# Block products of a Strassen FFN merged in TensorE's accumulators, and norms ahead of weights in the order of work

## The chip, the cores and the metric

The kernel runs on one core of a Trainium2 chip. The metric is the device time of one execution in microseconds (us): the median of three runs before is 1083.9 us (1083.37 to 1085.91). Five engines work side by side, each through a list of instructions of its own, in order: TensorE (PE; matmuls into accumulator tiles called `ps`), VectorE (DVE), ScalarE (ACT), GpSimd (POOL) and SyncE (SP, which issues DMAs). An instruction that needs the result of another engine waits for a semaphore.

## The reference

Two layers over 512 tokens of width 1024, in float32. Each layer has a mixer (attention and pooling in the first, a gated recurrence in the second) and then a SwiGLU FFN, both with a norm ahead and a norm behind:

```
D_MODEL = 1024; SEQ = 512; DEPTH = 2; D_FF = 2816

def rmsnorm(x, g):
    return x * lax.rsqrt(jnp.mean(x * x, axis=-1, keepdims=True) + RMS_EPS) * g

def swiglu(h, w_gate, w_up, w_down):
    return (jax.nn.silu(h @ w_gate) * (h @ w_up)) @ w_down

def reference(x, ...):
    for layer in range(DEPTH):
        h = rmsnorm(x, mix_pre_g[layer])
        m = even_mixer(h, ...) if layer % 2 == 0 else odd_mixer(h, ...)
        x = x + rmsnorm(m, mix_post_g[layer])
        h = rmsnorm(x, ffn_pre_g[layer])
        x = x + rmsnorm(swiglu(h, w_gate[layer], w_up[layer], w_down[layer]), ffn_post_g[layer])
    return x
```

## The kernel before, in words

**Precision.** Every float32 operand is split into a high and a low part, and a product is made of three matmuls (`mm3`: high x high, high x low, low x high). A unit of weights (128 x 1024) is loaded by SyncE into `raw`; ScalarE casts its high part into `whi`, and VectorE subtracts for the low part, `wlo` (`split_weights`). There are four buffers each of `whi` and `wlo`, used in turn.

**The FFN's first half.** The gate and up products are computed by a Strassen-Winograd scheme of 2 x 2 blocks: token blocks 0 and 1 against 2 and 3, and the two halves of the width. The normed and transposed tokens are kept in seven slots of features: `A11` and `A12` (blocks 0 and 1), `S1` to `S4` and `A22`, which need blocks 2 and 3. The output has `NP` = 11 tiles j, and each takes seven block products, one for each slot, with seven units of weights (some are sums of raw weights that VectorE makes). `gate_product` is one block product: 24 matmuls of 256 columns into one accumulator. The results are then merged by additions and subtractions (`y`, `z`, `c`), and `gated` forms silu(gate) x up out of each of the four quarters: a silu on ScalarE and a multiplication on VectorE.

For the first `LEAD` = 5 tiles A11 and A12 are computed early ("led"), while blocks 2 and 3 still go through the norm; the copy of A11's result is kept in a later part of `gs` meanwhile. Then the loop over all j computes S1, S2, (for j from 5 on A11 ahead of these and A12 behind S2), S3, S4 and A22.

**The norms.** `Finish` takes a mixer's output by token blocks of 128. `half` makes the squares on ScalarE (`Square`, with a sum) and the product with the gain on VectorE; `block` adds the residual and makes the squares for the next norm; `second`, some us later, the normed block `tmp`; `transpose`, later again, eight transposes on TensorE, whose results `Blocks.put` splits into the seven slots. `later(delay, ...)` and `tick` put these steps at a place in the program by a running count of matmul time; `need` waits for blocks.

**The order of work.** A scheduler orders each engine's instructions. What stands in `tc.high_priority` goes ahead of work that was written earlier, if its inputs are there by the scheduler's reckoning. Before the change only weights (loads, casts, splits, sums of raw weights) have it.

Lines of the profile that matter: L158 the cast to `whi`, L867 the copy of A11's result to `y`, L857 the silu, L705 the squares of `half`, L722 those of `block`, L743 the transposes, L136 to L138 the three matmuls of `mm3`. All of VectorE's instructions have line L100.

Of the kernel before, what the change touches and what calls it, by code (L numbers as in the profile page):

```python
# [15 lines left out]
P = 128  # L16
# [13 lines left out]
WINDOWS = (2, 4, 8, 16)  # L30
OUT_ORDER = (0, 1, 2, 7, 6, 5, 3, 4)


WARM = 8
ON_DVE = (0, 2)
# [29 lines left out]
def tile_trunk(ctx: ExitStack, tc: tile.TileContext, cst_d, sh_d, xw_d, x_d, gains_d, pw_d, w_d, out_d):  # L65
# [13 lines left out]
    def ps():  # L79
        return psp.tile([P, T], F32, name="ps", tag="ps")  # L80
# [29 lines left out]
    def tmp():  # L110
        return pc.tile([P, D], F32, name="tmp", tag="tmp", bufs=3)
# [6 lines left out]
    def later(delay, fn):  # L118
        pending.append((clock[0] + delay, fn))
        pending.sort(key=lambda p: p[0])  # L120
# [33 lines left out]
        return raw[:, :n]  # L154

    def split_weights(raw, hi, lo):
        with tc.high_priority():
            nc.scalar.copy(out=hi, in_=raw)  # L158
            vec.tensor_sub(out=lo, in0=raw, in1=f32(hi))

    def add_to(acc, other, eng):
        with tc.high_priority():
            eng.tensor_add(out=acc, in0=acc, in1=other)


# [473 lines left out]
    class Plain:  # L639


        def put(self, i, tps):
            for hf, tp in enumerate(tps):
                tv = tp.rearrange("p (k t) -> p k t", k=4)
                ks = slice(4 * hf, 4 * hf + 4)
                nc.scalar.copy(out=hBh[:, i, ks], in_=tv)
                vec.tensor_sub(out=hBl[:, i, ks], in0=tv, in1=f32(hBh[:, i, ks]))

    class Blocks:


        def put(self, i, tps):
            cs = slice(i % 2 * P, i % 2 * P + P)
# [29 lines left out]
    class Finish:  # L683
# [12 lines left out]
        def half(self, i, hf, acc, made_by=None):  # L696

            if i not in self.u:
                self.u[i] = (small(2), tmp())
            ss, u = self.u[i]  # L700
            cs = slice(hf * T, (hf + 1) * T)
            if made_by is not None:
                made_by(u[:, cs])
                acc = u[:, cs]
            nc.scalar.activation(out=junk[:, cs], in_=acc, func=AF.Square, scale=1.0 / 32, accum_out=ss[:, hf:hf + 1])  # L705
            vec.tensor_mul(out=u[:, cs], in0=acc, in1=self.gpost[:, cs])

        def block(self, i):
            ss, u = self.u.pop(i)
            gpre = self.gpre  # L710
            r = rstd(ss, 2)
            x = xres[i]
            halves = [slice(0, T), slice(T, D)]
            parts = halves if i == NB - 1 else [slice(0, D)]
            s2 = small(2)
            for q, cs in enumerate(parts):
                vec.scalar_tensor_tensor(out=x[:, cs], in0=u[:, cs], scalar=r, in1=x[:, cs], op0=ALU.mult,
                                               op1=ALU.add)
                if gpre is None:
                    nc.sync.dma_start(out=out_d[i * P:(i + 1) * P, cs], in_=x[:, cs])  # L720
                else:
                    nc.scalar.activation(out=junk[:, cs], in_=x[:, cs], func=AF.Square, scale=1.0 / 32,  # L722
                                         accum_out=s2[:, q:q + 1])
            if gpre is None:
                return
            box = {}

            def second():
                r2 = rstd(s2, len(parts))
                h = box["h"] = tmp()  # L730
                for cs in halves:
                    vec.scalar_tensor_tensor(out=h[:, cs], in0=x[:, cs], scalar=r2, in1=gpre[:, cs],
                                                   op0=ALU.mult, op1=ALU.mult)
                later(T1 if i < NB - 1 else T2, transpose)

            def transpose():
                h = box["h"]
                tps = []
                for hf in range(2):
                    tp = ps()  # L740
                    for b in range(4):
                        k = 4 * hf + b
                        nc.tensor.transpose(tp[:, b * P:(b + 1) * P], h[:, k * P:(k + 1) * P], ident)  # L743
                    tps.append(tp)
                self.sink.put(i, tps)
                made.add(i)

            made.discard(i)
            later(T3, second)
# [80 lines left out]
    def ffn(layer):  # L830
        st = ExitStack()
        pf = st.enter_context(tc.tile_pool(name=f"ffn{layer}", bufs=1, reuse_waits="tile"))
        upper[:] = [pf.tile([P, KT // 2 * D], F32R, name=f"up{n}") for n in range(2)]

        def ytile():
            return pf.tile([P, T], F32, name="y", tag="y", bufs=2)

        def gt(dt=F32):
            return pf.tile([P, 2, T], dt, name="g", tag="g", bufs=NP)


        gs = [gt() for _ in range(NP)]

        def gate_product(bank, w, f, more=False):
            wh, wl = w
            fh, fl = slot(f)
            for g in range(2):
                for k in range(4):
                    cs = slice(g * T + k * P, g * T + k * P + P)
                    ts = slice(k * 256, k * 256 + 256)  # L850
                    mm3(bank[:, g * 256:g * 256 + 256], wh[:, cs], wl[:, cs], fh[:, ts], fl[:, ts],
                        not more and g == 0 and k == 0, g == 1 and k == 3, 0.356, more)

        def gated(j, f, src, s):

            gate, up = src[:, :256], src[:, 256:]
            nc.scalar.activation(out=s, in_=gate, func=AF.Silu)  # L857
            cs = slice(f % 2 * 256, f % 2 * 256 + 256)
            vec.tensor_mul(out=gs[j][:, f // 2, cs], in0=s, in1=up)

        def first(j):

            b1 = ps()
            gate_product(b1, unit(), A11)

            y = gs[NP - 1 - j][:, 1] if j < LEAD else ytile()
            nc.scalar.copy(out=y, in_=b1)  # L867
            return b1, y

        def second(j, b1):  # L870
            gate_product(b1, unit(), A12, True)
            gated(j, 0, b1, tmp()[:, :256])

        led = []
        need(0, 1)
        for j in range(LEAD):
            led.append(first(j))
            second(j, led[j][0])
        need(2, 3)
        for j in range(NP):  # L880
            b1, y = led[j] if j < LEAD else first(j)
            z, c = hx[:, j % 2, :T], hx[:, j % 2, T:]
            b3 = ps()
            gate_product(b3, unit(), S1)
            b2 = ps()
            gate_product(b2, unit(), S2)
            vec.tensor_add(out=y, in0=b2, in1=y)
            vec.tensor_sub(out=z, in0=b3, in1=y)
            if j >= LEAD:
                second(j, b1)  # L890
            b4 = ps()
            gate_product(b4, unit(), S3)
            vec.tensor_sub(out=c, in0=z, in1=b4)
            gated(j, 3, c, c[:, :256])
            b5 = ps()
            gate_product(b5, unit(), S4)
            vec.tensor_add(out=z, in0=b5, in1=z)
            gated(j, 2, z, z[:, :256])
            gate_product(b4, unit(), A22, True)
            vec.tensor_add(out=y, in0=b4, in1=y)  # L900
            gated(j, 1, y, y[:, :256])


        def area(a):
            t = (hh, hl_) + tuple(upper)
            per = KT * T // D
            t = t[a // per]
            return tuple(t[:, a % per * D + n * T:a % per * D + n * T + T] for n in range(2))

        TAIL = 6  # L910
        early = [11, 15, 2, 6, 3, 7, 0, 4, 1, 5]
        areas = early + early[:FT - TAIL - len(early)] + [8, 12, 9, 13, 10, 14]
        parts = []

        def part(k, ahead=2):
            while len(parts) < min(FT, k + 1 + ahead):
                n = len(parts)
                src = gs[n // 2][:, n % 2]
                hi, lo = area(areas[n])
                nc.scalar.copy(out=hi, in_=src)  # L920
                vec.tensor_sub(out=lo, in0=src, in1=f32(hi))
                parts.append((hi, lo))
            return parts[k]

        for n in range(4):
            place[state["used"] + FT - TAIL + n] = lambda: tuple(gt(F32R).rearrange("p a t -> p (a t)") for _ in range(2))
        tm = TokenMajor([lambda k=k: part(k) for k in range(FT)], TAIL)
        tm.lead(range(3), (0, 1))
        tm.lead(range(3), (2, 3))
        tm.lead(range(3, FT - TAIL), range(NB))  # L930
        fin = Finish(1 if layer == 0 else 3, Plain())
        prefetch(TAIL + 2)
        tm.finish(range(NB), fin)
        st.close()
# [183 lines left out]
```

## Time and profile before

| | |
|---|---|
| median of three runs | 1083.9 us |
| the profiled execution's own time | 1087.36 us |
| its span, first to last instruction | 1085.6 us |
| TensorE busy | 1041.1 us, 96% |
| VectorE busy | 768.8 us, 71% |
| ScalarE busy | 516.9 us, 48% |
| mean granted clock of TensorE | 0.988 |

The busy share of an engine is a mean over stretches that differ. In the FFNs TensorE has no idle time for long stretches; in the transitions from mixer to FFN (about 190 to 240 us in layer 0, 720 to 760 us in layer 1) it waits for others. So a change has to be read stretch by stretch.

### The profile page before, as it was taken

The page shows a single profiled execution, that of the slowest core. Times are in us where ns is not written, and L with a number is a line of the kernel's source. Part 1 is how long each engine was busy: PE and PEld are TensorE (multiplying, and loading weights), DVE is VectorE, ACT ScalarE, POOL GpSimd, SP SyncE. Part 2 cuts the span into 40 slices and gives each one's busy share as a digit, 9 for nine tenths or more (in the row PEclk, how much of TensorE's full clock was granted, in tenths as well). Part 3 has the DMA queues.
Part 4 walks back from the last instruction along what each step waited for, and adds up shares of the span by engine and source line. Part 5 has one row for each costly group of instructions (what it writes and reads, how often), then busy time and mean ns, then how long its engine had stood idle before and what let it go on. Part 6 is the DMA issues. An engine that isn't in the chain of part 4 may idle for free. (4 is left out here: it accounts for less than half of the span.)

```text
span 1085.6 us, 16315 instructions
## 1 busy us (share of the span) xinstructions
PE 1041.1 (96%) x6558; PEld 931.0 (86%) x6558; DVE 768.8 (71%) x1045; ACT 516.9 (48%) x815; POOL 60.7 (6%) x96
## 2 busy tenths in 40 slices
PE   8989999789999999999999999897999999999997
PEld 6867777789999999888898887687999999988886
DVE  3778875788998989432357589468899889963313
ACT  6747644654444446332245894355444444542301
POOL 0020100100000000000012102210000000000000
PEclk9989999899999999999999999998999999999999
DMA  8563353232443244334123234132442432443201
GB/s 320 170 146 83 107 171 120 98 114 101 156 131 104 80 139 131 113 108 150 57 75 101 84 110 152 26 115 97 148 141 101 129 105 80 136 135 98 98 1 77
DMA packets 36188, 125.08 MB, mean 115 GB/s; under 512 B 4368, under 2 KB 4368, under 8 KB 36112
## 3 DMA queue, kind: packets, MB, share of 16 engines
q1 hardware_dynamic: 35536, 121.94, 35.6%
q10 hardware_dynamic: 576, 2.10, 0.5%
q8 instruction: 51, 0.84, 0.3%
q14 instruction: 25, 0.20, 0.1%
HBM read 117.73 MB, written 2.10 MB: 110 GB/s over the span
## 5 line engine op out<-in xcount | busy, mean ns | idle before, releaser
L158 ACT CAST whi<-raw 128x1024 fp32r<-128x1024 f32 x230 | 239.0, 1047 | 310.4 <-PE ps L137 113.1
L100 DVE TENSOR_TENSOR wlo<-raw,whi 128x1024 fp32r<-128x1024 f32 (+1 forms) x238 | 286.3, 1212 | 124.7 <-ACT whi L158 119.6
L136 PE MATMUL ps<-hTh,whi 128*128 128x256 f32 (+1 forms) x960 | 294.6, 307 | 5.5 <-ACT whi L158 2.5
L138 PE MATMUL ps<-hTh,wlo 128*128 128x256 f32 (+1 forms) x960 | 294.0, 307 | 3.8 <-DVE wlo L100 3.8
L137 PE MATMUL ps<-hTl,whi 128*128 128x256 f32 (+1 forms) x960 | 292.2, 305 | 3.5 <-DVE hTl L100 3.5
L136 PEld LDWEIGHTS ps<-hTh,whi 128*128 128x128 f32 x960 | 182.7, 190 | 15.0 <-ACT whi L158 3.1
L138 PEld LDWEIGHTS ps<-hTh,wlo 128*128 128x128 f32 x960 | 182.4, 190 | 13.3 <-DVE wlo L100 4.6
L137 PEld LDWEIGHTS ps<-hTl,whi 128*128 128x128 f32 x960 | 182.8, 190 | 12.2 <-DVE hTl L100 3.7
L136 PE MATMUL ps<-up,whi 128*128 128x256 f32 x528 | 149.8, 284 | 2.2 <-DVE hx L100 2.1
L137 PE MATMUL ps<-up,whi 128*128 128x256 f32 x528 | 149.4, 283 | 0.0
L138 PE MATMUL ps<-up,wlo 128*128 128x256 f32 x528 | 149.2, 283 | 0.0
L100 DVE TENSOR_TENSOR raw<-raw 128x1024 f32<-128x1024 f32 x88 | 106.9, 1220 | 8.1 <-DMA raw<-in_w 7.8
L136 PEld LDWEIGHTS ps<-up,whi 128*128 128x128 f32 x528 | 101.1, 191 | 3.1 <-DVE hx L100 3.0
L137 PEld LDWEIGHTS ps<-up,whi 128*128 128x128 f32 x528 | 101.2, 192 | 0.0
L138 PEld LDWEIGHTS ps<-up,wlo 128*128 128x128 f32 x528 | 101.1, 192 | 0.0
L100 DVE TENSOR_TENSOR tmp<-ps,gain 128x512 f32<-128x512 f32 x32 | 21.9, 690 | 59.0 <-ACT junk L705 58.9
L636 POOL TENSOR_TENSOR small<-small,nhalf 128x1 f32<-128x1 f32 x28 | 15.4, 549 | 800.1 <-DVE small L100 800.1
L137 PE MATMUL ps<-wlo,hTh 128*128 128x512 f32 (+2 forms) x160 | 55.8, 352 | 3.2 <-DVE wlo L100 3.1
L138 PE MATMUL ps<-whi,hTl 128*128 128x512 f32 (+2 forms) x160 | 55.5, 350 | 0.0
L136 PE MATMUL ps<-whi,hTh 128*128 128x512 f32 (+2 forms) x160 | 54.3, 351 | 0.6 <-ACT whi L303 0.6
L705 ACT ACTIVATE junk<-ps 128x512 bf16<-128x512 f32 x32 | 19.0, 596 | 60.7 <-PE ps L138 60.2
L138 PE MATMUL ps<-whi,hTh 128*128 128x512 f32 x96 | 38.0, 396 | 0.0
(220 smaller groups left out, 1655.3 us busy)
## 6 DMA issues: line engine op xcount, KB each, us to landing
raw<-in_w SPq DMA_DIRECT2D x200, 512.0 KB, 3.8
gain<-in_gains SPq DMA_DIRECT2D x7, 512.0 KB, 4.2
raw<-in_xw SPq DMA_DIRECT2D x6, 516.0 KB, 9.1
big<-in_x ACTq DMA_DIRECT2D x4, 512.0 KB, 7.8
big<-big SPq DMA_DIRECT2D x16, 128.0 KB, 4.2
xres<-in_x SPq DMA_DIRECT2D x4, 512.0 KB, 5.0
out_dram<-xres SPq DMA_DIRECT2D x3, 512.0 KB, 2.6
big<-tmp SPq DMA_DIRECT2D x8, 128.0 KB, 3.9
```

Of the source, the lines that this page charges most:

```text
L100: self.last = fn(*a, **k)
L136: nc.tensor.matmul(out, lhsT=ah, rhs=bh, start=start, stop=False, skip_group_check=more)
L137: nc.tensor.matmul(out, lhsT=ah, rhs=bl, start=False, stop=False, skip_group_check=more)
L138: nc.tensor.matmul(out, lhsT=al, rhs=bh, start=False, stop=stop, skip_group_check=more)
L158: nc.scalar.copy(out=hi, in_=raw)
L636: nc.gpsimd.tensor_tensor(out=r, in0=ms, in1=nhalf[:, :1], op=ALU.pow)
L705: nc.scalar.activation(out=junk[:, cs], in_=acc, func=AF.Square, scale=1.0 / 32, accum_out=ss[:, hf:hf + 1])
```

## The change

The merges move in part from VectorE into the accumulators. Two accumulators, `bw` and `bz`, are kept for the whole loop over j. ScalarE copies A11's result into `bw`, and S2 accumulates on it; ScalarE copies the negative of that into `bz`, and S3 and then A22 accumulate on `bw`, S4 on `bz`. VectorE keeps two merges of five for each j (`c` and `z`), ScalarE makes three copies (to `bw`, `bz`, `y`) in place of one, or of none for the led tiles, whose copy was made early. Two matmuls for each layer write the two accumulators once ahead of the loop. The norms of `Finish` get high priority, that of weights is set to 1500 places (`AHEAD`), and the transposes before an FFN are put 2.5 us later by the program's own count (`delay`).

```diff
+AHEAD = 1500
...
     def split_weights(raw, hi, lo):
-        with tc.high_priority():
+        with tc.high_priority(AHEAD):
...
     class Blocks:
+        delay = 2.5
...
         def half(self, i, hf, acc, made_by=None):
...
-            nc.scalar.activation(out=junk[:, cs], in_=acc, func=AF.Square, scale=1.0 / 32, accum_out=ss[:, hf:hf + 1])
-            vec.tensor_mul(out=u[:, cs], in0=acc, in1=self.gpost[:, cs])
+            with tc.high_priority():
+                nc.scalar.activation(out=junk[:, cs], in_=acc, func=AF.Square, scale=1.0 / 32,
+                                     accum_out=ss[:, hf:hf + 1])
+                vec.tensor_mul(out=u[:, cs], in0=acc, in1=self.gpost[:, cs])
         def block(self, i):
+            with tc.high_priority():
+                self._block(i)
...
-        led = []
         need(0, 1)
         for j in range(LEAD):
-            led.append(first(j))
-            second(j, led[j][0])
+            b1 = first(j)
+            nc.scalar.copy(out=gs[NP - 1 - j][:, 1], in_=b1)
+            second(j, b1)
         need(2, 3)
+        bw, bz = ps(), ps()
+        for b in (bw, bz):
+            nc.tensor.matmul(b, lhsT=junk[:, :P], rhs=junk[:, :T], start=True, stop=True)
         for j in range(NP):
-            b1, y = led[j] if j < LEAD else first(j)
-            z, c = hx[:, j % 2, :T], hx[:, j % 2, T:]
-            b3 = ps()
-            gate_product(b3, unit(), S1)
-            b2 = ps()
-            gate_product(b2, unit(), S2)
-            vec.tensor_add(out=y, in0=b2, in1=y)
-            vec.tensor_sub(out=z, in0=b3, in1=y)
+            if j < LEAD:
+                nc.scalar.copy(out=bw, in_=gs[NP - 1 - j][:, 1])
+            else:
+                b1 = first(j)
+                nc.scalar.copy(out=bw, in_=b1)
+            b5 = ps()
+            gate_product(b5, unit(), S1)
+            y = ytile()
+            nc.scalar.copy(out=y, in_=b5)
+            gate_product(bw, unit(), S2, True)
+            nc.scalar.mul(out=bz, in_=bw, mul=-1.0)
             if j >= LEAD:
                 second(j, b1)
-            b4 = ps()
-            gate_product(b4, unit(), S3)
-            vec.tensor_sub(out=c, in0=z, in1=b4)
+            z, c = hx[:, j % 2, :T], hx[:, j % 2, T:]
+            gate_product(bw, unit(), S3, True)
+            vec.tensor_sub(out=c, in0=y, in1=bw)
             gated(j, 3, c, c[:, :256])
-            b5 = ps()
-            gate_product(b5, unit(), S4)
-            vec.tensor_add(out=z, in0=b5, in1=z)
+            gate_product(bz, unit(), S4, True)
+            vec.tensor_add(out=z, in0=y, in1=bz)
             gated(j, 2, z, z[:, :256])
-            gate_product(b4, unit(), A22, True)
-            vec.tensor_add(out=y, in0=b4, in1=y)
-            gated(j, 1, y, y[:, :256])
+            gate_product(bw, unit(), A22, True)
+            gated(j, 1, bw, tmp()[:, :256])
```

**Where instructions stand, first place: the loop at j = 6, layer 0.** On ScalarE before, around the copy of A11's result (`y_3614` <- `ps_3582`); `whi_3648` and `whi_3679` are the weights of S3 and S4 of this j, and the second of these casts waits for S1's last matmul but one, which reads the buffer before:

```order
L857 ACTIVATE y_3385<-y_3385 128x256 [waits DVE_49]
L158 CAST whi_3648<-raw_3550 128x1024 [waits PE_49,Activation_49]
L867 COPY y_3614<-ps_3582 128x512 [waits PE_49]
L158 CAST whi_3679<-raw_3585 128x1024 [waits DMAHW1_49,PE_49,Activation_49]
L158 CAST whi_3711<-raw_3517 128x1024 [waits DVE_49,PE_49,Activation_49]
L158 CAST whi_3744<-raw_3746 128x1024 [waits DMAHW3_49,PE_49,Activation_49]
```

After, at the same place, with `whi_3644` and `whi_3674` for S3 and S4; `ps_2521` is `bw`, `ps_2522` is `bz`:

```order
L870 ACTIVATE tmp_3575<-ps_2521 128x256 [waits PE_49]
L160 CAST whi_3644<-raw_3546 128x1024 [waits PE_49,Activation_49]
L160 CAST whi_3674<-raw_3581 128x1024 [waits DMAHW1_49,PE_49,Activation_49]
L900 COPY ps_2521<-ps_3578 128x512 [waits DVE_49,Activation_49]
L904 COPY y_3642<-ps_3611 128x512 [waits PE_49]
L160 CAST whi_3705<-raw_3513 128x1024 [waits PE_49]
L907 ACTIVATE ps_2522<-ps_2521 128x512 [waits PE_49,Activation_49]
```

The copy to `bw` stands behind both casts, where the copy to `y` stood between them. On TensorE before, where S1 ends (`ps_3616`) and S2 begins (`ps_3647`); the waits at S2 are for its weights:

```order
L138 MATMUL ps_3616<-hTh_65,wlo_3549 128x256
L136 MATMUL ps_3616<-hTh_65,whi_3548 128x256
L137 MATMUL ps_3616<-hTl_66,whi_3548 128x256
L138 MATMUL ps_3616<-hTh_65,wlo_3549 128x256
L136 MATMUL ps_3647<-hTh_65,whi_3583 128x256 [waits Activation_49]
L137 MATMUL ps_3647<-hTl_66,whi_3583 128x256
L138 MATMUL ps_3647<-hTh_65,wlo_3584 128x256 [waits DVE_49]
```

After, S2 accumulates in `ps_2521`:

```order
L140 MATMUL ps_3611<-hTh_65,wlo_3545 128x256
L138 MATMUL ps_3611<-hTh_65,whi_3544 128x256
L139 MATMUL ps_3611<-hTl_66,whi_3544 128x256
L140 MATMUL ps_3611<-hTh_65,wlo_3545 128x256
L138 MATMUL ps_2521<-hTh_65,whi_3579 128x256 [waits Activation_49]
L139 MATMUL ps_2521<-hTl_66,whi_3579 128x256
L140 MATMUL ps_2521<-hTh_65,wlo_3580 128x256
```

S2's one wait for ScalarE is now one for the copy to `bw`.

**Second place: a led tile, j = 2 of layer 0.** On ScalarE before, where the casts follow each other (`whi_2886` for S4 and `whi_2917` for A22 of this j, `whi_2952` for S1 of the next):

```order
L158 CAST whi_2856<-raw_2789 128x1024 [waits PE_49,Activation_49]
L158 CAST whi_2886<-raw_2823 128x1024 [waits DMAHW1_49,PE_49,Activation_49]
L158 CAST whi_2917<-raw_2787 128x1024 [waits DVE_49,PE_49,Activation_49]
L857 ACTIVATE hx_67<-hx_67 128x256 [waits DVE_49]
L158 CAST whi_2952<-raw_2954 128x1024 [waits PE_49]
L857 ACTIVATE hx_67<-hx_67 128x256 [waits DVE_49]
L857 ACTIVATE g_2141<-g_2141 128x256 [waits DVE_49]
```

After: `whi_2890` and `whi_2919` are the weights of S4 and A22 of this j, `whi_2953` those of S1 of the next, `ps_2858` is S1's accumulator, `g_2140` holds A11's result:

```order
L160 CAST whi_2890<-raw_2825 128x1024 [waits DMAHW1_49,PE_49]
L870 ACTIVATE tmp_2854<-ps_2521 128x256 [waits PE_49]
L160 CAST whi_2919<-raw_2789 128x1024 [waits PE_49,Activation_49]
L904 COPY y_2888<-ps_2858 128x512 [waits PE_49]
L897 COPY ps_2521<-g_2140 128x512 [waits DVE_49]
L160 CAST whi_2953<-raw_2955 128x1024 [waits PE_49]
L907 ACTIVATE ps_2522<-ps_2521 128x512 [waits PE_49,Activation_49]
L160 CAST whi_2989<-raw_2955 128x1024 [waits DVE_49,PE_49]
```

The copies to `y` and to `bw` stand behind one cast, the copy to `bz` behind the next.

**Third place: the norm of block 3 in layer 0.** On ScalarE before; `xres_1833` is the residual of block 3, `whi_2262` and `whi_2323` are weights of led products:

```order
L158 CAST whi_2204<-raw_2206 128x1024 [waits DMAHW7_49,PE_49]
L705 ACTIVATE junk_68,small_2092<-ps_1949 128x512
L867 COPY g_2142<-ps_2143 128x512 [waits PE_49]
L722 ACTIVATE junk_68,small_2121<-xres_1833 128x512 [waits DMAHW4_49,DVE_49,Activation_49]
L158 CAST whi_2262<-raw_2264 128x1024 [waits DMAHW0_49,PE_49]
L158 CAST whi_2323<-raw_2325 128x1024 [waits DMAHW1_49,PE_49]
L722 ACTIVATE junk_68,small_2121<-xres_1833 128x512 [waits DVE_49,Activation_49]
```

After:

```order
L712 ACTIVATE junk_68,small_2092<-ps_1948 128x512 [waits PE_49,Activation_49]
L712 ACTIVATE junk_68,small_2092<-ps_1949 128x512 [waits PE_49]
L674 COPY hx_67<-ps_2051 128x4x128 [waits DVE_49]
L160 CAST whi_2204<-raw_2206 128x1024 [waits DMAHW7_49,PE_49]
L888 COPY g_2142<-ps_2143 128x512 [waits PE_49]
L734 ACTIVATE junk_68,small_2121<-xres_1833 128x512 [waits DMAHW4_49,DVE_49,Activation_49]
L734 ACTIVATE junk_68,small_2121<-xres_1833 128x512 [waits DVE_49,Activation_49]
L160 CAST whi_2262<-raw_2264 128x1024 [waits DMAHW0_49,PE_49]
```

The second half's squares have moved ahead of both casts. On VectorE after, the rows up to the split of block 3's S1 slot, `hTl_66<-tmp_2321`:

```order
L102 TENSOR_TENSOR wlo_2420<-raw_2421,whi_2419 128x1024 [waits DMAHW4_49,PE_49,Activation_49]
L102 TENSOR_TENSOR tmp_2244<-tmp_2245,hx_67 128x512
L102 TENSOR_TENSOR up1_2131<-tmp_2244,up0_2130 128x4x128
L102 TENSOR_TENSOR g_2133<-tmp_2292,ps_2203 128x256
L102 TENSOR_TENSOR wlo_2454<-raw_2455,whi_2453 128x1024 [waits PE_49,Activation_49]
L102 TENSOR_TENSOR up1_2131<-tmp_2244,up0_2130 128x4x128 [waits Activation_49]
L102 TENSOR_TENSOR raw_2455<-raw_2455,raw_2489 128x1024 [waits DVE_49]
L102 TENSOR_TENSOR raw_2623<-raw_2623,raw_2625 128x1024 [waits DMAHW4_49,DMAHW3_49]
L102 TENSOR_TENSOR tmp_2321<-ps_2311,tmp_2321 128x512 [waits Activation_49]
L102 TENSOR_TENSOR tmp_2322<-hx_67,ps_2311 128x512
L102 TENSOR_TENSOR wlo_2488<-raw_2455,whi_2487 128x1024 [waits PE_49,Activation_49]
L102 TENSOR_TENSOR hTl_66<-tmp_2321,hTh_65 128x4x128 [waits Activation_49]
```

Splits of weights (`wlo`) and sums of raw weights stand in the rows ahead of it.

## Rows read from the trace of the kernel before

**Rows 1.** The page, part 1: busy time of each engine and its share of the span.

```profile
PE 1041.1 (96%) x6558; PEld 931.0 (86%) x6558; DVE 768.8 (71%) x1045; ACT 516.9 (48%) x815; POOL 60.7 (6%) x96
```

**Rows 2.** Windows of 20 us: busy time of each engine, granted clock.

```profile
core 0: us, PE busy (x) PEld busy (x) DVE busy (x) ACT busy (x) POOL busy (x), PEclk, DMA share, GB/s
200.00:220.00 20.00, 14.66 (x106) 14.24 (x105) 16.11 (x24) 12.45 (x24) 1.65 (x3) 0.83 0.38 132
220.00:240.00 20.00, 16.30 (x133) 15.48 (x132) 19.66 (x26) 9.74 (x14) 0.00 (x0) 1.00 0.34 105
360.00:380.00 20.00, 20.00 (x171) 20.00 (x170) 17.33 (x21) 8.99 (x13) 0.00 (x0) 1.00 0.32 105
```

**Rows 3.** TensorE's waits, whole run: who for whom, us in total, times, longest.

```profile
PE ps L743 <- DVE tmp L100: 7.5, 5, 4.9
PE ps L136 <- ACT whi L158: 5.1, 4, 2.6
PE ps L137 <- DVE wlo L100: 4.4, 2, 3.1
PE ps L138 <- DVE wlo L100: 3.8, 4, 1.5
PE ps L137 <- DVE hTl L100: 3.5, 1, 3.5
```

**Rows 4.** Timeline of ScalarE in layer 0 at j = 7: start, duration, instruction, idle time before.

```profile
356.17 0.40 ACT L857 ACTIVATE y<-y 128x256 f32<-128x256 f32 x1
...
357.20 1.05 ACT L158 CAST whi<-raw 128x1024 fp32r<-128x1024 f32 x1 [0.63 <-PE ps L137]
...
358.15 0.58 ACT L867 COPY y<-ps 128x512 f32<-128x512 f32 x1
...
360.01 1.05 ACT L158 CAST whi<-raw 128x1024 fp32r<-128x1024 f32 x1 [1.28 <-issue]
```

**Rows 5.** Timeline of TensorE there: S1's matmul before its last, and S2's first.

```profile
359.65 0.28 PE L137 MATMUL ps<-hTl,whi 128*128 128x256 f32 x1
...
359.89 0.28 PE L136 MATMUL ps<-hTh,whi 128*128 128x256 f32 x1
```

**Rows 6.** Timeline of VectorE there: a weight sum, two splits of weights.

```profile
357.31 1.22 DVE L100 TENSOR_TENSOR raw<-raw 128x1024 f32<-128x1024 f32 x1
...
358.44 1.22 DVE L100 TENSOR_TENSOR wlo<-raw,whi 128x1024 fp32r<-128x1024 f32 x1
...
361.09 1.23 DVE L100 TENSOR_TENSOR wlo<-raw,whi 128x1024 fp32r<-128x1024 f32 x1 [0.76 <-ACT whi L158]
```

**Rows 7.** One form of the merges on VectorE, all 24 of its kind.

```profile
L100 DVE TENSOR_TENSOR y<-ps,y 128x512 f32<-128x512 f32 x24 | 16.6, 691 | 5.9 <-PE ps L138 5.9
```

**Rows 8.** What TensorE waited for from 260 to 300 us.

```profile
PE ps L136 <- DVE hx L100: 1.3, 2, 0.8
PE ps L138 <- DVE wlo L100: 0.8, 1, 0.8
PE ps L136 <- ACT whi L158: 0.4, 1, 0.4
```

**Rows 9.** Timeline of ScalarE, VectorE and TensorE around block 3's norm, layer 0.

```profile
206.81 1.97 ACT L158 CAST whi<-raw 128x1024 fp32r<-128x1024 f32 x2
...
208.69 0.62 ACT L722 ACTIVATE junk<-xres 128x512 bf16<-128x512 f32 x1
...
210.96 1.42 DVE L100 SCALAR_TENSOR_TENSOR tmp<-xres,small,gain 128x512 f32<-128x512 f32 x2 [0.66 <-POOL small L636]
...
211.86 1.51 PE L743 MATMUL ps<-ident,tmp 128*128 128x128 f32 x6 [4.94 <-DVE tmp L100]
...
225.96 0.68 DVE L100 TENSOR_TENSOR hTl<-tmp,hTh 128x512 fp32r<-128x512 f32 x1
...
227.32 0.39 PE L136 MATMUL ps<-hTh,whi 128*128 128x256 f32 x1 [1.08 <-ACT whi L158]
```

**Rows 10.** Matmuls of 512 columns, a group by form.

```profile
L137 PE MATMUL ps<-wlo,hTh 128*128 128x512 f32 x96 | 38.0, 395 | 0.0
```

More of the change, by code (lines that the diff above doesn't have):

```diff
@@ L161, in add_to @@
     def add_to(acc, other, eng):
-        with tc.high_priority():
+        with tc.high_priority(AHEAD):
             eng.tensor_add(out=acc, in0=acc, in1=other)
@@ L639, in tile_trunk @@
     class Plain:
+        delay = 0.0
         def put(self, i, tps):
@@ L704, in half, with _block @@
                 acc = u[:, cs]
-            nc.scalar.activation(out=junk[:, cs], in_=acc, func=AF.Square, scale=1.0 / 32, accum_out=ss[:, hf:hf + 1])
-            vec.tensor_mul(out=u[:, cs], in0=acc, in1=self.gpost[:, cs])
+            with tc.high_priority():
+                nc.scalar.activation(out=junk[:, cs], in_=acc, func=AF.Square, scale=1.0 / 32,
+                                     accum_out=ss[:, hf:hf + 1])
+                vec.tensor_mul(out=u[:, cs], in0=acc, in1=self.gpost[:, cs])
         def block(self, i):
+            with tc.high_priority():
+                self._block(i)
+        def _block(self, i):
             ss, u = self.u.pop(i)
@@ L728, in second @@
             def second():
[L729 to L734, printed above, removed]
+                with tc.high_priority():
+                    r2 = rstd(s2, len(parts))
+                    h = box["h"] = tmp()
+                    for cs in halves:
+                        vec.scalar_tensor_tensor(out=h[:, cs], in0=x[:, cs], scalar=r2, in1=gpre[:, cs],
+                                                       op0=ALU.mult, op1=ALU.mult)
+                later((T1 if i < NB - 1 else T2) + self.sink.delay, transpose)
             def transpose():
@@ L864, in first @@
             gate_product(b1, unit(), A11)
-            y = gs[NP - 1 - j][:, 1] if j < LEAD else ytile()
-            nc.scalar.copy(out=y, in_=b1)
-            return b1, y
+            return b1
         def second(j, b1):
```

## The prediction

> **What bounds the kernel now.** The page's first part comes first: TensorE is busy 1041.1 of 1085.6 us [rows 1]. In the windows the FFN's stretch from 360 to 380 us shows TensorE at 20.00 of 20, VectorE at 17.33 and ScalarE at 8.99 [rows 2]: there every wait of TensorE lengthens the run, and time freed on VectorE shortens nothing. The windows 200:220 and 220:240, the transition from mixer to FFN in layer 0, are different: TensorE 14.66 and 16.30, VectorE 19.66 of 20 in the second [rows 2]. The view of TensorE's waits says how much it could win back: its five costliest kinds make 7.5 + 5.1 + 4.4 + 3.8 + 3.5 = 24.3 us in the whole run [rows 3]. That bounds any gain, since the change leaves the number of block products as it was.
>
> The last view is the timeline where S1 of j = 7 ends, in layer 0. S1's last matmul but one starts at 359.65, S2's first at 359.89 with no idle time [rows 5]; ScalarE's next cast of weights starts at 360.01 [rows 4]. Four `whi` buffers serve the products in turn, so this cast writes S4's weights into the buffer that S1 held, and waits for that last matmul but one. Casts therefore start 2.8 us apart (357.20, 360.01), one at each product's end.
>
> **What the change costs, part by part.**
>
> *Merges, j of 6 to 10.* VectorE loses three 128x512 merges of 0.691 us per j [rows 7]. With VectorE at 17.33 of 20 and TensorE full, I take that at nothing. S2 now accumulates in `bw`, so its first matmul waits for ScalarE's copy of `b1` into `bw`, and every later matmul queues behind it. In the order of work the cast of S4's weights stands ahead of that copy; ScalarE works in order, and the cast waits for S1 to be all but over. From the moment at which S2 could start (359.89): 0.12 until the cast starts (360.01), 0.95 until ScalarE can start its next instruction (357.20 to 358.15), the copy 0.58 [rows 4, 5], and 0.03 for the handover, as from the cast's end at 361.06 to VectorE's split at 361.09 [rows 6]. That is 1.68 us idle per j, five times in each layer: 8.4 us a layer. For j = 5 the copy stands ahead of the cast, and I take nothing.
>
> No row shows ScalarE writing an accumulator. The nearest is its copy out of one, 0.58 [rows 4]; its floor is nothing, its ceiling the 1.05 of a cast twice as long [rows 4]. With these a stall would be 1.1 or 2.15; I take 0.58, the same tile. The copy to `bz` needs 0.95 + 0.58 after S2, and `c` one merge of 0.69; A12 and S4 stand between and last 2.8 each, so both hide for j from 5 on. Were that cover gone, they would cost (0.58 + 0.03) on 12 products and (0.69 + 0.03) on 22, some 23 us.
>
> On this a page has an opinion. The Trainium skill, "Perfetto Trace Analysis", section "Matmuls", says that independent groups of matmuls should rotate through the banks, so that one bank's evacuation overlaps the next group. The change puts S2, S3 and A22 into one bank; by that rule alone all three reuses wait, and the sum would be 23 us higher than mine. The trace of before, with a bank for each, shows no idle time at S2; it cannot show what A12 and S4 hide.
>
> *Merges, the products led (j below 5).* Their A11 and A12 ran early, so nothing stands between S2 and S3, except two matmuls of the next S1. Two stalls follow for j = 1 to 4. (a) S2 waits as above; for j = 2 and 3 the copy of S1's result to `y` stands ahead as well, which adds 0.58 less the 0.10 that neighbours overlap (1.05 against 0.95 [rows 4]), so 2.16. In layer 0, j = 1 is worse: the `bw` copy waits until VectorE has read the old `bw`, and ahead of that multiplication stand a split that waits for the cast, a raw sum and another multiplication: 0.12 + 1.08 + 1.13 + 1.13 + 0.4 + 0.4 + 0.6 = 4.9, with 1.13 from one VectorE operation to the next (357.31 to 358.44 [rows 6]) and 0.4 estimated for 256 columns from the 0.69 for 512 [rows 7]. (b) S3 waits for `bz`, made behind a cast that waits for S2's last matmul but one: 0.12 + 0.95 + 0.58 + 0.03, less 0.24 for two matmuls (359.65 to 359.89 [rows 5]): 1.44, four times, 5.8 in a layer. Layer 0: 4.9 + 2 x 2.16 + 1.68 + 5.8 = 16.7, less the 1.3 + 0.8 + 0.4 = 2.5 that TensorE waits there already [rows 8]: 14.2. Layer 1: j = 1 and 4 at 1.68, 2 and 3 at 2.16, with (b) 13.5; its j = 0 adds 2.1 (no early matmuls, and a silu of 0.40 [rows 4] in the way: 0.12 + 0.95 + 0.40 + 0.58 + 0.03): 15.6.
>
> *Norms ahead of weights.* In layer 0 the second Square of block 3 stood behind two casts (206.81 to 208.69), which made the norm's last product late (210.96); TensorE idled 4.94 us before the transposes at 211.86 [rows 9]. The order now has the Square ahead of both casts, so these transposes come some 5 us sooner. What is late next is S1 of j = 0: it needs the split of block 3's S1 slot, which VectorE made at 225.96 for a start at 227.32 [rows 9]. In the new order seven weight splits and four raw sums stand between the norm and that split: 11 x 1.13 = 12.4, and 14 smaller operations of some 0.6, 8.4; from 206, together 226.8. So S1 starts as before, with A12 of j = 2 (2.8) done by then and about 1.2 of the waits in the 220 to 240 window gone: −4, between −7 (all of the norm's lead) and −2. In layer 1 the order of the norms is nearly unchanged up to the last transposes: 0.
>
> *Small things.* GpSimd's order is the same, and on SyncE's queue two loads of raw weights change places, both issued well ahead of their use: nothing. The transposes, put 2.5 us later by the program's own count, stand behind nine more matmuls, 9 x 0.12 us that TensorE has to do anyway (0.24 for two [rows 5]): nothing. The last block's norm no longer waits for one gain multiplication: −0.6, nearest row 0.69 [rows 7]. Four extra matmuls of 512 columns: 0 to 4 x 0.395 [rows 10], I take 0.7. Clock: in 200:220, with the idle 4.94, the mean grant was 0.83; that is 0.17 x 20 / 0.5 = 6.8 us at the lower level, up to 3.4 us of matmul time; 220:240, with four pauses of about one us, kept 1.00 [rows 2, 9]. A pause of 4.9 returns at j = 1 of layer 0: I take 2 once, of 0 to 3.4.
>
> **The sum.** Layer 0: −4 + 14.2 + 8.4 = 18.6. Layer 1: 15.6 + 8.4 = 24.0. With −0.6 + 0.7 + 2: +44.7 us. The profiled execution took 1087.36, 3.5 above the median of the runs; it would take 1132.1, and the median goes from 1083.9 to 1128.6.
>
> **Rivals.**
> 1. *Only one family of stalls comes.* Should ScalarE reach the led copies in time because VectorE, relieved, feeds it sooner, −4 + 8.4 + 8.4 and the small terms leave +14: 1098. Should only the led stalls come, +28: 1112. For it: VectorE was the full engine there (19.66). Against: each stall begins with a cast that waits for TensorE itself, whatever VectorE does.
> 2. *The clock falls.* Led products idle twice within 5 us, about 3.5 us in 18; if each of eight loses up to 3.4: up to +27, 1131 to 1156. For it: 200:220. Against: 220:240 idled as much in pieces at 1.00. The Trainium skill, "TensorE: Matmul & The Clock Gate", section "A second HAM failure mode: psum-queue depth-cycling", tells of short idles between groups that cycle through banks making the clock oscillate; by it this rival would be the likeliest, and 220:240 disagrees so far.
> 3. *Every reuse of the bank waits*: +23, 1152. Against it: A12 and S4 between.
> 4. *Faster.* If the `bw` copy were never late, the transitions would decide. That needs the cast to start 1.53 us (0.95 + 0.58) before S1's last matmul but one, so a free `whi` buffer; then the gain is at most 24.3 and 6.8 of clock [rows 2, 3]: 1060 to 1080. A row of the order speaks against it at each j.
>
> **Chances.** Forecast (1112 to 1135) 0.60; rival 1 0.14; rival 2 0.13; rival 3 0.03; rival 4 0.06; the rest, stalls offset to no change, 0.04. The range 1100 to 1150 leaves out rival 4, no change, part of rival 1 and the far ends of 2 and 3, under 2 in 10. This kernel's measurement tells changes over 0.3% from none: faster 0.06, same 0.03, slower 0.91.
>
> **What would show it.** TensorE's waits should list ScalarE's copies: `bw` nine or ten times a layer, nearly 1.7 us each, and `bz` four or five times. A 20 us window in the FFN should hold about 18.4 of TensorE, not 20.00; S1 of j = 0 should start near 227 us. I am wrong if S2 starts at once behind S1, if the casts start before S1's end, or if the clock stays low through the led products.

## The result, and the profile after

The changed kernel takes 1137.05 us (median of 4 runs, 1135.74 to 1138.45) against 1084.91 us for the kernel before (1083.37 to 1086.27): a ratio of 1.0481, 95% interval 1.0459 to 1.0504. The forecast was 1128.6, range 1100 to 1150. The profiled execution took 1135.74 us over a span of 1133.7, 48.1 us more than the span before.

The page, part 1, of the changed kernel (busy time, share of the span), which answers to [rows 1]:

```profile
PE 1057.2 (93%) x6560; PEld 939.8 (83%) x6562; DVE 731.9 (65%) x979; ACT 542.4 (48%) x869; POOL 65.5 (6%) x96
```

TensorE has 16 us more busy time for the same number of products (some of it at a lower clock, as the windows show), and its share falls from 96% to 93%. VectorE is relieved by 37 us, and the run is longer all the same. The windows of the changed kernel, to set against [rows 2]:

```profile
220.00:240.00 20.00, 15.42 (x113) 14.81 (x114) 15.47 (x20) 10.36 (x17) 0.00 (x0) 0.91 0.27 87
240.00:260.00 20.00, 14.90 (x116) 14.52 (x115) 15.33 (x20) 8.55 (x13) 0.00 (x0) 0.92 0.38 132
260.00:280.00 20.00, 17.03 (x126) 16.34 (x126) 12.80 (x14) 7.72 (x11) 0.00 (x0) 0.91 0.28 84
280.00:300.00 20.00, 16.93 (x130) 16.34 (x129) 12.82 (x14) 7.71 (x11) 0.00 (x0) 0.95 0.40 125
360.00:380.00 20.00, 18.45 (x156) 18.25 (x155) 15.10 (x17) 8.55 (x13) 0.00 (x0) 1.00 0.29 89
980.00:1000.00 20.00, 18.16 (x141) 17.96 (x140) 16.30 (x22) 13.39 (x22) 0.00 (x0) 0.91 0.32 104
```

From 360 to 380 us TensorE has 18.45 of 20 where it had 20.00, at a clock of 1.00: idle time, not slower matmuls. From 220 to 300 us, the led tiles, it has 14.9 to 17.0, and the clock is 0.91 to 0.95. What TensorE waited for in the changed kernel (in total, times, longest), beside [rows 3]:

```profile
PE ps L138 <- ACT ps L897: 18.0, 8, 5.1
PE ps L138 <- ACT ps L900: 16.0, 10, 1.8
PE ps L138 <- ACT whi L160: 10.4, 9, 2.5
PE ps L138 <- ACT g L888: 6.6, 6, 2.3
...
PE ps L138 <- ACT ps L907: 2.2, 1, 2.2
```

The first two rows are the copies to `bw`, at led tiles (L897) and from j = 5 on (L900); neither existed before. L888 is the copy of a led A11 result to `gs`, L160 the cast, L907 the copy to `bz`. The timeline of the changed kernel at j = 7 of layer 0 shows one such wait:

```profile
373.02 1.22 DVE L102 TENSOR_TENSOR raw<-raw 128x1024 f32<-128x1024 f32 x1
...
374.16 1.22 DVE L102 TENSOR_TENSOR wlo<-raw,whi 128x1024 fp32r<-128x1024 f32 x1
...
375.55 0.28 PE L140 MATMUL ps<-hTh,wlo 128*128 128x256 f32 x1
375.63 0.41 DVE L102 TENSOR_TENSOR g<-tmp,ps 128x256 f32<-128x256 f32 x1
375.79 1.04 ACT L160 CAST whi<-raw 128x1024 fp32r<-128x1024 f32 x1 [1.77 <-PE ps L139]
376.75 0.58 ACT L900 COPY ps<-ps 128x512 f32<-128x512 f32 x1
...
377.38 0.39 PE L138 MATMUL ps<-hTh,whi 128*128 128x256 f32 x1 [1.55 <-ACT ps L900]
```

S1's last matmul starts at 375.55, so S2 could start at 375.67. The cast starts at 375.79, the copy to `bw` at 376.75, S2 at 377.38: 1.71 us late. But one row was not in the forecast: VectorE's read of `bw`, the last product of j = 6, starts at 375.63 and ends at 376.04. It stands behind a raw sum and a split of weights. The copy could not have started before that, cast or no cast. The cast ends later still, so in this kernel it sets the 1.71.

Where the 48 us arise is read from the starts of the same matmul, the first of S3, at j = 5 and j = 10 of both layers. Timeline of TensorE before:

```profile
325.65 0.28 PE L136 MATMUL ps<-up,whi 128*128 128x256 f32 x1
...
425.38 0.28 PE L136 MATMUL ps<-up,whi 128*128 128x256 f32 x1
...
848.71 0.28 PE L136 MATMUL ps<-up,whi 128*128 128x256 f32 x1
...
948.45 0.28 PE L136 MATMUL ps<-up,whi 128*128 128x256 f32 x1
```

and after:

```profile
339.63 0.27 PE L138 MATMUL ps<-up,whi 128*128 128x256 f32 x1
...
448.70 0.28 PE L138 MATMUL ps<-up,whi 128*128 128x256 f32 x1
...
886.58 0.27 PE L138 MATMUL ps<-up,whi 128*128 128x256 f32 x1
...
997.15 0.28 PE L138 MATMUL ps<-up,whi 128*128 128x256 f32 x1
```

| stretch | forecast | measured |
|---|---|---|
| start to S3 of j = 5, layer 0 | −4 + 14.2 + 2 + 0.35 = +12.6 | 339.63 − 325.65 = +14.0 |
| S3 of j = 5 to S3 of j = 10, layer 0 | +8.4 | 109.07 − 99.73 = +9.3 |
| from there to S3 of j = 5, layer 1 | 15.6 + 0.35 = +16.0 | 437.88 − 423.33 = +14.6 |
| S3 of j = 5 to S3 of j = 10, layer 1 | +8.4 | 110.57 − 99.74 = +10.8 |
| from there to the end | −0.6 (the last block's norm) | 136.55 − 137.15 = −0.6 |

The 0.35 are the two extra matmuls ahead of each layer's loop. In all the forecast adds 44.7 us, and the spans of the profiled executions differ by 48.1.

### The profile page after: what moved, and what is told of

It reads as the page before. It is cut to its first block, busy times and chain, and to the rows that moved or that the text cites. A ratio compares the mean times of both kernels' runs of the same rounds, so it can differ in the third digit from the quotient of the medians.

```text
span 1133.7 us, 16343 instructions
## 1 busy us (share of the span) xinstructions
PE 1057.2 (93%) x6560; PEld 939.8 (83%) x6562; DVE 731.9 (65%) x979; ACT 542.4 (48%) x869; POOL 65.5 (6%) x96
## 5 line engine op out<-in xcount | busy, mean ns | idle before, releaser
L160 ACT CAST whi<-raw 128x1024 fp32r<-128x1024 f32 x230 | 239.3, 1047 | 347.4 <-PE ps L139 175.3
L138 PE MATMUL ps<-hTh,whi 128*128 128x256 f32 (+1 forms) x960 | 301.2, 314 | 53.0 <-ACT ps L897 18.0
L139 PE MATMUL ps<-hTl,whi 128*128 128x256 f32 (+1 forms) x960 | 296.3, 309 | 1.0 <-DVE hTl L102 1.0
L138 PEld LDWEIGHTS ps<-hTh,whi 128*128 128x128 f32 x960 | 185.7, 194 | 69.6 <-ACT ps L897 19.6
L140 PEld LDWEIGHTS ps<-hTh,wlo 128*128 128x128 f32 x960 | 186.1, 194 | 10.0 <-DVE wlo L102 1.3
L139 PEld LDWEIGHTS ps<-hTl,whi 128*128 128x128 f32 x960 | 186.2, 194 | 9.8 <-DVE hTl L102 1.2
```

Source lines behind the costliest of these rows:

```text
L138: nc.tensor.matmul(out, lhsT=ah, rhs=bh, start=start, stop=False, skip_group_check=more)
L139: nc.tensor.matmul(out, lhsT=ah, rhs=bl, start=False, stop=False, skip_group_check=more)
L140: nc.tensor.matmul(out, lhsT=al, rhs=bh, start=False, stop=stop, skip_group_check=more)
```

## The experiments

Theory B, formed on the trace after, says that a stall at S2 has two queues behind it: VectorE reads `bw`'s last product late, behind work on weights, and ScalarE's copy stands behind a cast. The expectation below calls it their sum; as the copy waits for both, it is the later of the two that sets the stall. The rivals: A, the cast alone (the forecast's theory); C, the new order of norms and weights makes the loss; D, a bank that is used again is slow whatever the order.

**One bank, copy ahead of the cast** (e1_copy_first). `behind` maps a unit of weights to the copy behind which its cast has to stand:

```diff
+            cast = nc.scalar.copy(out=hi, in_=raw)
+        if state["loaded"] in behind:
+            order(cast, behind[state["loaded"]])
...
+                cp = nc.scalar.copy(out=bw, in_=b1)
+            behind[state["used"] + 4] = cp
             b5 = ps()
             gate_product(b5, unit(), S1)
             y = ytile()
-            nc.scalar.copy(out=y, in_=b5)
+            order(nc.scalar.copy(out=y, in_=b5), cp)
```

(and the same for the led tiles' copy).

> The changed kernel with ScalarE's copy to bw put ahead of the cast of weights behind which it stood, by an order of the two instructions, still one bank. Theory A, the cast alone makes the stall: all stalls at S2 vanish, 17.5 us in the loops from j = 6 and some 19 us at the led tiles, to about 1101 us. Theory B, the cast and the single bank together: in the trace of the changed kernel VectorE ended reading bw's last product at 376.04, while S2 could have started at 375.67; then 0.37 + 0.03 + 0.58 + 0.03 = 1.0 us of each 1.7 stays, and the run gains 10 x 0.7 = 7 us there and some 3 us at the led tiles: about 1127 us. Theory C, the new order of norms and weights makes the loss: no change from 1137 us.

Measured: 1122.61 us, ratio to before 1.0348 (1.0310 to 1.0385). Its timeline at j = 7:

```profile
370.05 0.28 PE L140 MATMUL ps<-hTh,wlo 128*128 128x256 f32 x1
370.13 0.41 DVE L102 TENSOR_TENSOR g<-tmp,ps 128x256 f32<-128x256 f32 x1
370.65 0.57 ACT L904 COPY ps<-ps 128x512 f32<-128x512 f32 x1 [2.12 <-DVE g L102]
371.13 1.05 ACT L160 CAST whi<-raw 128x1024 fp32r<-128x1024 f32 x1
...
371.27 0.39 PE L138 MATMUL ps<-hTh,whi 128*128 128x256 f32 x1 [0.95 <-ACT ps L904]
```

The copy now starts right behind VectorE's read and ahead of the cast. S1's last matmul starts at 370.05, so S2 could start at 370.17, and starts at 371.27: 1.10 late. A had 1101 us and no stall, C no change; B had 1.0 us left and 1127, and is the nearest. The cast alone is not the cause.

**Two banks** (e2_two_banks).

```diff
-        bw, bz = ps(), ps()
-        for b in (bw, bz):
+        bws, bzs = (ps(), ps()), (ps(), ps())
+        for b in bws + bzs:
...
         for j in range(NP):
+            bw, bz = bws[j % 2], bzs[j % 2]
```

> The changed kernel with two banks each for bw and bz, used by even and odd j. The order of ScalarE then has the copy to bw ahead of the cast, since it no longer waits for the reading of the product before. Theories A and B: no stall at S2, 17.5 + 19 us less, about 1101 us, while the stalls at S3 of the led tiles (1.2 us each, eight) stay. Theory C: no change from 1137 us. A third, that a product accumulating on copied data is slow in itself: no change either, with matmuls farther apart than 0.12 us.

Measured: 1091.15 us, ratio 1.0056 (1.0034 to 1.0077): 46 of the 52 us come back, 10 more than expected. Those 10 are other waits and the clock: TensorE's waits for copies to `gs` (L888) fall from 6.6 to 2.2 us, and 40 matmuls of the FFNs run at the lower clock in place of 96, some 5 us (how they are counted stands with the clock below). The window from 360 to 380 us:

```profile
360.00:380.00 20.00, 20.00 (x171) 20.00 (x170) 15.37 (x17) 9.94 (x16) 0.00 (x0) 1.00 0.34 107
```

TensorE is at 20.00 again. VectorE is at 15.37, 2.0 us under the 17.33 of before [rows 2], and that is worth nothing, since TensorE was full in both. No wait for a copy to `bw` is left in the list of waits. C is out. What is left of the loss lies mostly at the led tiles, where the second bank changes nothing for S3:

```profile
PE ps L138 <- ACT whi L160: 11.1, 9, 2.6
```

Eight of these nine waits, about 1.0 each, are where S3 of a led tile comes next (1.2 in the expectation; see the led tiles below). The kernel before with the new order alone (e3_norms_only) has one wait for such a cast, 2.5 us.

**One bank, read first and copy first** (e5_read_and_copy_first): as e1_copy_first, and

```diff
-            gated(j, 1, bw, tmp()[:, :256])
+            with tc.high_priority(2 * AHEAD):
+                gated(j, 1, bw, tmp()[:, :256])
```

> As e1_copy_first, one bank still, and VectorE's multiplication that reads bw's last product of a j goes ahead of the splits and raw sums that stood before it. Theory B, the stall at S2 is the sum of two queues (the read behind VectorE's work on weights, the copy behind ScalarE's cast), and one bank is no cost in itself: the 1.0 us that e1_copy_first still shows at each S2 from j = 6 goes, and most of the 0.7 to 2.8 at the led tiles: 1088 to 1095 us, like e2_two_banks. Theory D, a bank that is used again is slow whatever the order: no change from 1123 us.

Measured: 1101.85 us, ratio 1.0131 (1.0095 to 1.0166), beside 1.0348 for the copy alone. Its window and the list of waits:

```profile
360.00:380.00 20.00, 20.00 (x171) 20.00 (x170) 15.42 (x18) 9.94 (x15) 0.00 (x0) 1.00 0.33 106
```

```profile
PE ps L138 <- ACT ps L901: 6.1, 7, 2.0
```

From j = 6 on no stall is left: one bank costs nothing there if its reader and its copy stand in the right place, so D is out for these. The 1088 to 1095 us expected were too low: at the led tiles seven waits for the copy remain, 6.1 us in sum. There S2 of j + 1 follows A22 of j with one product between them in place of two. The copy of j = 2 in this kernel's timeline of ScalarE:

```profile
272.75 0.59 ACT L901 COPY ps<-g 128x512 f32<-128x512 f32 x1 [1.34 <-DVE g L102]
273.27 1.05 ACT L160 CAST whi<-raw 128x1024 fp32r<-128x1024 f32 x1
```

It waits 1.34 us for VectorE's read, with no cast ahead of it. With a second bank (e2_two_banks) no such wait is left.

**The two parts of the change by themselves** (e3_norms_only: the priorities and the delay in the kernel before; e4_merges_only: the merges with the priorities and the delay of before).

```diff
-        with tc.high_priority():
+        with tc.high_priority(AHEAD):
...
+            with tc.high_priority():
+                self._block(i)
...
-                later(T1 if i < NB - 1 else T2, transpose)
+                later((T1 if i < NB - 1 else T2) + self.sink.delay, transpose)
```

> The kernel before with the new priorities, those of norms and of weights, and the later transposes, but its own merges. Theories A and B: the merges cost all, so about the time before or the 1 to 4 us less that the transition of layer 0 gains: 1081 to 1085 us. Theory C: most of the 52 us, about 1130 us.

> The changed kernel with the priorities and the transposes of the kernel before, so the new merges alone. Theories A and B: the same stalls, about 1137 to 1141 us. Theory C: about the time before, 1085 to 1095 us.

Measured: the norms only 1078.02 us, ratio 0.9916 (0.9885 to 0.9948); the merges only 1134.06 us, ratio 1.0463 (1.0411 to 1.0515). So the merges cost all, and the new order alone is a gain, twice what was expected of it. Two things stand in that order, the norms' high priority and the weights' 1500 places; no run has one without the other, so which of them gains is not shown. In e3_norms_only:

```profile
203.09 1.42 DVE L101 SCALAR_TENSOR_TENSOR tmp<-xres,small,gain 128x512 f32<-128x512 f32 x2 [0.66 <-POOL small L637]
...
221.85 0.38 PE L137 MATMUL ps<-hTh,whi 128*128 128x256 f32 x1 [2.51 <-ACT g L879]
...
226.48 0.38 PE L137 MATMUL ps<-hTh,whi 128*128 128x256 f32 x1 [1.54 <-ACT hTh L665]
```

Block 3's normed tile is made at 203.09 in place of 210.96 [rows 9], and the wait of 4.94 is gone; S1 of j = 0 starts at 226.48, late for ScalarE's cast of its slot; its next matmul waits another 0.96 us for VectorE's split of it, whose lateness was the forecast (226.8). TensorE did led work in the time won. A new wait, 2.51, is for ScalarE's copy to `g`. The whole change (1.0481) is not faster than its merges alone (1.0463, 1.0411 to 1.0515): by the intervals no more than some 4 of the 8 us can be left once the merges are there. The list of waits of e4_merges_only tells a part of where, and its timeline at S2 of j = 1, layer 0:

```profile
PE ps L138 <- ACT ps L894: 14.4, 8, 2.1
...
PE ps L753 <- DVE tmp L102: 7.5, 5, 4.9
```

```profile
254.46 0.39 PE L138 MATMUL ps<-hTh,whi 128*128 128x256 f32 x1 [1.55 <-ACT ps L894]
```

Its longest wait at a led copy (L894) is 2.1 us, 5.1 in the changed kernel (the row L897 above), and it does wait 4.9 for the transposes. The 5.1 is at j = 1 of layer 0 (rows further below), behind VectorE's work on weights, of which the changed order puts more ahead of that read: a split and a raw sum, where e4_merges_only has a split alone and the wait is 1.55. Why the scheduler orders VectorE so was not taken apart.

**Two variants of the norms.** e6_norms_no_delay has `delay = 0.0`; e7_norms_g_copies_first puts the led copies ahead of casts, as in e1_copy_first:

```diff
+            cp = nc.scalar.copy(out=y, in_=b1)
+            if j < LEAD:
+                behind[state["used"] + 4] = behind[state["used"] + 5] = cp
```

> e3_norms_only with the transposes where they stood (delay 0 in place of 2.5). If the earlier squares alone bring the 8 us: 1078 us. If the transposes' place has a part in it, TensorE waits again for block 3's normed tile, up to the 4.9 us of before: 1079 to 1083 us.

> e3_norms_only with ScalarE's copies of the led A11 results put ahead of the casts behind which they stood. In e3_norms_only TensorE waits 5.7 us for these copies, 2.5 in each layer at one place. If they go and nothing else comes late: 1073 us. If S1 of j = 0 then waits for VectorE's split of block 3 instead, as forecast for layer 0: 1077 to 1078 us.

Measured: 1079.70 us, ratio 0.9930 (0.9906 to 0.9954), and 1076.91 us, ratio 0.9897 (0.9863 to 0.9932). All three (with e3_norms_only) are faster than both kernels, by 0.7 to 1.0%; the intervals don't tell them apart. In the first the wait of 4.94 for block 3's tile does not come back (its longest wait for such a tile is 0.8), so the delay is not what removed it. In the second, a wait moved rather than went:

```profile
PE ps L137 <- ACT g L883: 8.4, 7, 3.2
```

These waits are 8.4 us in all, where e3_norms_only had 5.7: in each layer the wait of 2.5 fell to 0.6, and a new one of 3.2 stands some 10 us later.

## Why the prediction was right, and where not

The sign, the bound and the main stalls came as forecast. The median, 1137.05, is 8 us above the forecast, inside the range and 2 us outside the band 1112 to 1135 that had the chance 0.60. The transition and the clock were mis-sized.

**Bound and sign: right.** In the loop from j = 6 on TensorE was full (20.00 of 20 from 360 to 380 us [rows 2]), so an idle pause in each j adds in full, and VectorE's relief is worth nothing: the window of e2_two_banks shows it.

**The stall at S2 from j = 6: size right, cause half right.** Forecast 0.12 + 0.95 + 0.58 + 0.03 = 1.68, measured 1.71, with each piece of the sum in the rows above. The step that failed is that one queue was priced: by rival 4 the copy would not be late if only the cast began earlier ("needs the cast to start 1.53 us (0.95 + 0.58) before S1's last matmul but one"). The forecast named VectorE's read for j = 1 of layer 0 only, and from j = 6 on took the cast alone, though the read stood in the same row of the order ("[waits DVE_49,Activation_49]"). Shown by e1_copy_first and e5_read_and_copy_first: 1.71 us with both late, 1.10 with the read late, none with neither. The size came out because the cast was the later of the two here. The fourth case, the read early and the copy behind the cast, was not run.

**The rule on banks.** The Trainium skill, "Perfetto Trace Analysis", section "Matmuls", would have independent groups of matmuls rotate through banks. The forecast took from it a wait at each of three reuses and set that aside, but for S2 and the led tiles. Rotation from one j to the next brought back 46 of 52 us (e2_two_banks), so the rule was the better guide to the mend. Within one j the products S2, S3 and A22 build on each other and are no independent groups; there the waits at S3 of the led tiles stay with two banks. The +23 us of rival 3 did not come: from j = 5 on, where A12 and S4 stand between, no row shows a wait for `bz` or for the readers of `bw` at A22. The one wait put down to `bz` (L907, 2.2 us) is at j = 0 of layer 1, forecast at 2.1.

**The price of a copy into an accumulator: right.** A row by form of the changed kernel:

```profile
L907 ACT ACTIVATE ps<-ps 128x512 f32<-128x512 f32 x22 | 12.8, 581 | 0.0
```

0.58, as out of one (0.578 before); the copies to `bw` take 0.58 and 0.59 (L900, L897).

**The led tiles: right within 2 us in each layer.** The longest wait, at j = 1 of layer 0, in the timeline of the changed kernel:

```profile
253.99 1.22 DVE L102 TENSOR_TENSOR wlo<-raw,whi 128x1024 fp32r<-128x1024 f32 x1
255.12 1.22 DVE L102 TENSOR_TENSOR raw<-raw 128x1024 f32<-128x1024 f32 x1
256.26 0.42 DVE L102 TENSOR_TENSOR g<-hx 128x256 f32<-128x256 f32 x1
256.59 0.41 DVE L102 TENSOR_TENSOR g<-tmp,ps 128x256 f32<-128x256 f32 x1
...
257.23 0.58 ACT L897 COPY ps<-g 128x512 f32<-128x512 f32 x1
...
257.87 0.58 PE L138 MATMUL ps<-hTh,whi 128*128 128x256 f32 x1 [5.10 <-ACT ps L897]
...
259.74 0.41 PE L140 MATMUL ps<-hTh,wlo 128*128 128x256 f32 x1
259.95 0.41 PE L138 MATMUL ps<-hTh,whi 128*128 128x256 f32 x1
```

A split, a raw sum and a multiplication stand ahead of the read at 256.59, as forecast; 4.9 was the sum, and TensorE idles 5.10. The second stall of the led tiles, S3 behind the copy to `bz`, came too. At j = 2 of layer 0:

```profile
281.09 0.28 PE L140 MATMUL ps<-hTh,wlo 128*128 128x256 f32 x1
...
282.24 0.58 ACT L907 ACTIVATE ps<-ps 128x512 f32<-128x512 f32 x1
...
282.87 0.39 PE L138 MATMUL ps<-up,whi 128*128 128x256 f32 x1
```

S2's last matmul starts at 281.09; with two matmuls of the next S1 between, S3 could start at 281.45, and starts at 282.87, right behind the copy to `bz`: 1.42 late, forecast 1.44. The list of waits has these eight stalls under the cast (row L160), as the two matmuls between wait for the same cast that stands ahead of the copy.

**The transition: the term −4 was too large.** The FFN's first matmul and the first of S2 of j = 1, layer 0, before:

```profile
196.74 0.28 PE L136 MATMUL ps<-hTh,whi 128*128 128x256 f32 x1
...
256.38 0.28 PE L136 MATMUL ps<-hTh,whi 128*128 128x256 f32 x1
```

and the FFN's first after:

```profile
194.38 0.40 PE L138 MATMUL ps<-hTh,whi 128*128 128x256 f32 x2
```

By S2 of j = 1 both kernels have done the same products of the FFN. From the FFN's first matmul that takes 59.64 us before; after, S2 starts at 257.87, less its own wait of 5.10 at 252.77, which is 58.39. So the change gains some 1.3 us here, not 4. Another 2.4 in the table's first row are there before the FFN begins; e4_merges_only, with the old order of norms, has 3.6 at the same place, so they can't be put down to the norms. The wait of 4.94 for block 3 is gone, as forecast, but most of it was given back. What was not costed is that A12 of a led tile waits for ScalarE's copy to `gs`, which stands behind casts: row L888, two of its six waits, 2.28 and 1.55 us, here. S1 of j = 0 starts at 225.15, 2 us before the forecast's 227, and waits once more for VectorE's split, until 226.49. The gain of 8 us in e3_norms_only is for the most part not of this transition either: by the starts of its matmuls 1.5 lie here and 3.5 at the led tiles j = 1 to 4 of layer 0.

**The clock: too small.** 2 us was taken. From 220 to 300 us the granted clock of the changed kernel is 0.91, 0.92, 0.91 and 0.95; before, it was 0.83 from 200 to 220 and 1.00 from 220 to 240 [rows 2]. The starts of neighbouring matmuls tell the cost: 0.21 us apart at the lower level of 1.2 GHz (259.74 and 259.95, behind the pause of 5.10), 0.12 at the upper. Counted so over the trace, 35 matmuls of the FFNs run at the lower level before and 96 after, each 0.095 us longer: 3.3 and 9.1 us. So the change costs some 6 us by the clock, 4 more than was taken: rival 2 came in a small part. The sum of 44.7, with 4 more for the clock, 2.7 more for the transition and the 2.4 ahead of the FFN taken off, is 49.0, beside the 48.1 measured; that the last two nearly cancel is luck. Layer 1's last stretch exceeds its five stalls by 2 us, with one window at 0.91 (980 to 1000, the last row of the windows above). The page "TensorE: Matmul & The Clock Gate" of the Trainium skill, section "A second HAM failure mode: psum-queue depth-cycling", tells of short idles between groups that cycle through banks making the clock oscillate; here drops came behind such pauses in the led windows and once at j = 10 of layer 1 (a pause of 1.84 us), and not in 360 to 380 us, with a pause of 1.55. Why the one and not the other is open.

## What to carry to other kernels

Read all the waits of an instruction on an engine that works in order, and price what stands ahead of it and ahead of each engine that it waits for: the later of the queues sets the stall, and to mend one alone moves it to the other. Where a product accumulates on copied data, give the accumulator a second bank before moving instructions about; the copy's own 0.58 us was never the trouble. Test the parts of a change apart: here a loss of 52 us hid that one part, alone, gains 8.

## What was not expected of the hardware

Nothing in the engines themselves. A matmul that accumulates on what ScalarE wrote runs as one that starts afresh (TensorE 20.00 of 20 in e2_two_banks and e5_read_and_copy_first, as before), and ScalarE writes an accumulator in the 0.58 us in which it reads one.
